# Two-layer hybrid trunk on one core: split weights get buffers 64 bytes longer, and start at the beginning or 64 bytes on, by stage

## The chip, the core and the metric

The kernel runs on one core of a Trainium2 chip, as one launch. The metric is the device time of one execution in microseconds (us). Before the change, three runs took 753.79, 753.91 and 755.08 us; the median is 753.91 us.

## What is computed

The input x is 256 tokens by 1024 features. Two layers follow each other, each of two sublayers. Cut to what matters:

```python
def hybrid_mixer(x, w_in, w_branch_sb, w_branch_moba, w_out):
    proj = x @ w_in                     # q,k,v of 8 + 8 heads, and two gates
    ...
    branch_sb = merge_heads(o_sb) @ w_branch_sb
    branch_mb = merge_heads(o_mb) @ w_branch_moba
    merged = jax.nn.sigmoid(g_sb) * branch_sb + jax.nn.sigmoid(g_mb) * branch_mb
    return merged @ w_out

for l in range(DEPTH):                  # 2
    mix = hybrid_mixer(x, ...)
    x = layer_norm(DEEPNORM_ALPHA * x + mix, ...)
    ffn = (silu(x @ w_gate) * (x @ w_up)) @ w_down      # 2816 wide
    x = layer_norm(DEEPNORM_ALPHA * x + ffn, ...)
```

Everything is float32. The matrix products work on pairs of float32r parts: a value is split into hi (rounded) and lo (the rest), and a product is hi·hi + hi·lo + lo·hi, three matmuls.

## The kernel before

**Weights.** All weights of a layer lie in HBM as 122 granules of 128 x 1024 float32, in the order of use (`_granules`). `WeightStream` brings them in one by one: a DMA from the SP queue into one of 4 raw buffers (`load`), a cast on ScalarE into `whi` (line 48), a subtraction on VectorE into `wlo` (line 53). There are 10 buffers for `whi` and 10 for `wlo` (`NSPLIT`); granule g takes the buffers that granule g - 10 has left. Every use of a granule is a set of `mm3` calls, three matmuls each, all recorded at line 275.

**Stages of a layer, by granule** (the names are those of the accumulators in PSUM, after l0 or l1):

- 0 to 7: `pv`, `pq` (in layer 1 both are called `pvq`), token-major. x is the stationary operand, 128 x 128, and a granule's 512 columns move through.
- 8, 9, 14, 15, 20, 21, 24, 25: `pqk`; 22, 23 and 26 to 39: `pg` (gates). Feature-major: the granule is stationary, 128 x 128, and x moves, 256 tokens wide (`feat_major`).
- 10 to 13 `pk` and 16 to 19 `pu`: token-major, 512 columns of weights move.
- 40 to 47: `pb`, the branch projections, feature-major: the granule is stationary, the attention output o moves, 256 wide.
- 48 to 55: `pw`, the output projection: m is stationary, 512 columns of weights move.
- 56 to 63: `pft`, the first chunks of SwiGLU, token-major, 512 columns move.
- 64 to 99: `pf`, the rest of SwiGLU, feature-major, x moves, 256 wide: 36 granules, 864 matmuls a layer.
- 100 to 121: the down projection, `pd` (and `pe` in layer 1): h is stationary, 512 columns of weights move, in two of `pe`'s banks 256.

The token-major stages on x (`pv`, `pq` or `pvq`, `pk`, `pu`, `pft`) have 288 matmuls a layer, `pb` has 192.

**Order.** Every engine takes its instructions in program order. `Weave` writes that order: the main line is the matmuls above, and side lines (attention heads, norms, rotary, the splits of the weights) are put between them by an estimate of when their operands are there. So matmuls of attention (`sb_s`, `mb_s`, `sb_o`, `mb_o`) and transposes (`pT`, `tp`, `sg..T`, line 288) interrupt the runs of projections at fixed places of the program.

**Where things lie.** A partition of SBUF is filled pool after pool, in the order in which the pools and their tiles are declared, each tile rounded up to 32 bytes. In the built program the constants begin at byte 16512 (129 x 128) with `ident` (512 bytes), `rope` (256), `x0` and `x1` (4096 each), `xT_hi` and `xT_lo` (8192 each) and `mask` (1024): all begin on a multiple of 128 bytes, x transposed (`xT_hi`, `xT_lo`) at 25472 and 33664. Then come `zero` and `mhalf`, 32 bytes each. So all that follows begins 64 bytes past a multiple of 128: the raw buffers from 42944, `whi` from 59328, `wlo` from 100288, and from 141248 the activations (o, m, h, q, k, v), 4096 bytes each. Slices inside a buffer are steps of 512 bytes and more. Call the first 64 bytes of each aligned 128 the lower half and the others the upper half: x transposed begins in the lower half, all weights and those activations begin in the upper half.

Of the kernel before, what the change touches and what calls it, by code (L numbers as in the profile page):

```python
# [8 lines left out]
F32R = mybir.dt.float32r  # L9
# [5 lines left out]
P = 128  # L15
# [14 lines left out]
GCOLS = 1024  # L30
NG_LAYER = 122
# [3 lines left out]
class Weave:  # L35
    """Program order: the main line of projections, with side lines (attention, norms,
    rotary, weight splits) woven in. Every engine takes its instructions in program order,
    so each is emitted about when its operands are there, by an estimate of the time at
    which each engine gets through what it has been given. A side line yields the time
    at which it goes on; on the tensor engine's clock."""  # L40

# [40 lines left out]
    def start(self, gen):  # L82
        """A side line whose first stage comes now."""
        side = self.add(gen)
        if not self.busy:
            self._step(side)
        return side
# [9 lines left out]
class WeightStream:  # L97
    """Weight granules [128, 1024]: loaded in float32, then split exactly into
    two float32r parts (hi = rounded, lo = the rest) for the tensor engine."""

# [13 lines left out]
    def load(self, upto):  # L114
        while self.loaded < min(upto, self.total):
# [7 lines left out]
            self.loaded += 1  # L123

    def line(self):
        """The side line: a granule at a time, as far as the buffers allow."""
        nc, weave = self.nc, self.weave
        while self.split < self.total:
            g = self.split
            ahead = g - self.current  # L130
            if g > self.limit:
                yield weave.t + 0.1
                continue
            if ahead >= LEAD and max(weave.dve_t, weave.act_t) > weave.t + BACKLOG:
                yield weave.t + 0.2
                continue
            self.load(g + NRAW)
            if ahead > 0:
                yield self.there[g]
            hi, lo = (self.pool.tile([P, GCOLS], F32R, tag=n, name=f"{n}{g}", bufs=NSPLIT)  # L140
                      for n in ("whi", "wlo"))
            t = self.raw.pop(g)
            n = GCOLS // len(self._pieces(g))
            for sl in self._pieces(g):
                e = weave.act(self.there[g], n, nc.scalar.copy, hi[:, sl], t[:, sl])
            if g - self.current > 0:
                yield e
            for sl in self._pieces(g):
                e = weave.dve(e, n, nc.vector.tensor_sub, lo[:, sl], t[:, sl], hi[:, sl].bitcast(F32))
            self.parts[g], self.ready[g] = (hi, lo), e  # L150
            self.split += 1
            self.load(g + 1 + NRAW)

    def allow(self, g):
        """Granule g's buffers are free from here on."""
        self.limit = max(self.limit, min(g, self.total - 1))
# [9 lines left out]
NRAW = 4  # L166
NSPLIT = 10
HOLD = 8
N_WARM = 7
# [10 lines left out]
def hybrid_trunk_kernel(ctx: ExitStack, tc: tile.TileContext, w, xT_in, x_in, ln_in,  # L180
# [6 lines left out]
    work = ctx.enter_context(tc.tile_pool(name="work", bufs=3))  # L187
# [24 lines left out]

# [1 line left out]
    xT_raw = [unit(f"xT_raw{t}", [P, KC, P]) for t in range(2)]  # L214
# [12 lines left out]
    nc.scalar.activation(warm, zero, AF.Sigmoid)  # L227
    # The tensor engine's clock rises after some microseconds of work: give it zeros meanwhile.
    idle = unit("idle", [P, 512], F32R)
# [42 lines left out]

# [1 line left out]
    def mm(o, a, b, start, stop):  # L274
# [30 lines left out]
    def tok_major(o, g, t, first, last, k0):  # L305
        """o[tokens of t, 512] += x @ granule g ([2 kc, 512])."""
        hi, lo = ws.take(g)
        hi = hi.rearrange("p (k c) -> p k c", k=2)
        lo = lo.rearrange("p (k c) -> p k c", k=2)
        for k in range(2):  # L310
            ts = slice(t * P, (t + 1) * P)
            mm3(o, xT_hi[:, k0 + k, ts], xT_lo[:, k0 + k, ts], hi[:, k, :], lo[:, k, :],
                first and k == 0, last and k == 1)

    def both_tokens(name, g0, put):
        """All tokens of x @ granules g0..g0+3; put(tokens, bank) takes each half."""
        acc = [bankM(f"{name}{t}", [P, WIDTH]) for t in range(2)]
        order = ((0, 0), (1, 0), (0, 1), (1, 1), (0, 2), (0, 3)) if g0 == 0 else \
            ((0, 0), (0, 1), (0, 2), (1, 0), (1, 1), (0, 3))
        for t, k in order + ((1, 2), (1, 3)):  # L320
            tok_major(acc[t], g0 + k, t, k == 0, k == 3, 2 * k)
            if t == 1:
                ws.allow(g0 + k + NSPLIT)
            if k == 3:
                put(t, acc[t])

    def feat_major(o, g):
        """o[128 columns, 256 tokens] = (x @ granule g)^T, g [8 kc, 128 columns]."""
        hi, lo = ws.take(g)
        hi = hi.rearrange("p (k c) -> p k c", k=KC)  # L330
        lo = lo.rearrange("p (k c) -> p k c", k=KC)
        for k in range(KC):
            mm3(o, hi[:, k, :], lo[:, k, :], xT_hi[:, k, :], xT_lo[:, k, :], k == 0, k == KC - 1)
        ws.allow(g + NSPLIT)

    def token_out(o, g, t, s_hi, s_lo, first, last):
        """o[tokens of t, 1024] += s^T @ granule g ([1 kc, 1024]); o: (first column, bank) ..."""
        hi, lo = ws.take(g)
        ts = slice(t * P, (t + 1) * P)
        for c0, ps in o:  # L340
            cs = slice(c0, c0 + ps.shape[-1])
            mm3(ps, s_hi[:, ts], s_lo[:, ts], hi[:, cs], lo[:, cs], first, last)

    ROWS = [(slice(h * DH, (h + 1) * DH), slice((1 - h) * DH, (2 - h) * DH)) for h in range(2)]

    # Per head, q is stacked as [hi; lo] over the 128 rows and each part of k is there twice,
    # so that q k^T = q_stack (k_hi twice) + q_stack (k_lo twice).
    def stack_q(qs, src, n, c, e):
        """qs[head] [128, ...] from src [2 heads x 64, ...]; the second head is [lo; hi]."""
        for h, (a, b) in enumerate(ROWS):  # L350
            e = act(e, n, nc.scalar.activation, qs[h][a], src[a], AF.Copy, scale=c)
        yield e
        for h, (a, b) in enumerate(ROWS):
            dve(e, n, nc.vector.scalar_tensor_tensor, qs[h][b], src[a], c, qs[h][a].bitcast(F32),
                op0=OP.mult, op1=OP.subtract)
# [15 lines left out]
    def rope_line(name, ps, t, put):  # L371
        """Token-major q or k (8 heads x 64) -> rotary -> transposed, handed to put."""
        tmp = work.tile([P, 8, DH], F32, tag="T", name=f"{name}_tok{t}")
# [22 lines left out]
    def scores(s, q, kh, kl, m):  # L396
        """Scores of both heads of a pair: columns 0:128 = (q0, k0), 128:384 = (q1, k0 k1),
        with the causal mask m added to the diagonal blocks."""
        for h in range(2):
# [12 lines left out]
    def weighted(name, p, wt, v, oT, e):  # L412
        """oT[:, p] = (wt @ v)^T for both heads of pair p."""
        yield e + MARGIN
# [93 lines left out]
    def scale_shift(e, x, cols, sub, op, scale, g, b, e_scale):  # L508
        """x <- ((x op sub) g) scale + b; yields each piece of columns as it is done."""
        for c in cols:  # L510
# [7 lines left out]
    def norm_line(name, t, junk, gb):  # L518
        """x_t <- LN(alpha x_t + ps) g + b, and its transpose into xT (split)."""
        x = xs[t]  # L520
# [26 lines left out]
    def last_norm(name, t, banks, gb, down):  # L547
        """The output's tokens: LN(alpha x_t + sum) g + b, blocks of columns in turn."""
        x = xs[t]
# [24 lines left out]

# [1 line left out]
    norms = []  # L576
    for l in range(DEPTH):
        G = l * NG_LAYER
        L = f"l{l}"

        # v of stick-breaking and q of MoBA: tokens 0..127 first
        v_sb = pair_tiles(L + "vsb", [P, 2, WIDTH])
# [28 lines left out]

        # Each pair of stick-breaking heads starts with its q and k; k and v of MoBA and the
        # first gates come between, MoBA's heads after the last sigmoid of stick-breaking, and
        # the gates' sigmoids after the last exponential of MoBA.
        o_sb = pair_tiles(L + "osb", [P, NPAIR, S])
# [47 lines left out]

        # branch projections and the gated merge, feature-major
        gb = load_gb(l, 0)
# [20 lines left out]

        # output projection: tokens 0..127 first
        norms = []
# [7 lines left out]

        # SwiGLU, first chunks token-major (tokens 0..127 first)
        h_t = [pair_tiles(f"{L}h{i}", [P, 4, S]) for i in range((NFC + 3) // 4)]
# [47 lines left out]

        # down projection: the last granules' tokens 0..127 first
        gb = load_gb(l, 1)
# [108 lines left out]
```

## Time and profile before

| | |
|---|---|
| runs | 753.79, 753.91, 755.08 us; median 753.91 |
| profiled execution, span from first to last instruction | 747.6 us |
| median of the runs less that span | 6.3 us |
| instructions | 12689, of these 5049 matmuls |
| matmul time that the page shows as busy | 735.1 us, 98% of the span |
| VectorE, ScalarE busy | 71%, 56% |
| share of the chain of waits that is matmul | 84% |

The profile gives the span, and no separate time of the execution around it. A matmul's own duration in it holds its way through the array (276 to 283 ns for 256 columns); as matmuls follow each other in a pipeline, the pace is read from the distance of their starts. In the chain of waits a piece such as "143.10 23.02 PE l0pb L275 x192" gives the start, the duration and the number of the matmuls in it, and duration by number is the pace.

### The profile page before, as it was taken

The page shows a single profiled execution, that of the slowest core. Times are in us where ns is not written, and L with a number is a line of the kernel's source. Part 1 is how long each engine was busy: PE and PEld are TensorE (multiplying, and loading weights), DVE is VectorE, ACT ScalarE, POOL GpSimd, SP SyncE. Part 2 cuts the span into 40 slices and gives each one's busy share as a digit, 9 for nine tenths or more (in the row PEclk, how much of TensorE's full clock was granted, in tenths as well). Part 3 has the DMA queues.
Part 4 walks back from the last instruction along what each step waited for, and adds up shares of the span by engine and source line. Part 5 has one row for each costly group of instructions (what it writes and reads, how often), then busy time and mean ns, then how long its engine had stood idle before and what let it go on. Part 6 is the DMA issues. An engine that isn't in the chain of part 4 may idle for free.

```text
span 747.6 us, 12689 instructions
## 1 busy us (share of the span) xinstructions
PE 735.1 (98%) x5049; PEld 675.5 (90%) x5049; DVE 529.9 (71%) x772; ACT 421.8 (56%) x655; POOL 13.4 (2%) x20
## 2 busy tenths in 40 slices
PE   8999999999999999999999999999999999999996
PEld 5888999998799999988888889999987999999885
DVE  6897878696886666644488878886768866665416
ACT  6788867744565445433267877777435654554300
POOL 0000000000000000000000000000010000000001
PEclk9999999999999999999999999999999999999999
DMA  8864724554586565676168445345635865657501
GB/s 292 284 217 151 221 93 153 176 199 167 178 265 227 181 194 182 198 241 194 60 196 258 146 162 177 108 145 198 210 113 183 277 201 194 196 185 246 166 1 56
DMA packets 39082, 136.31 MB, mean 182 GB/s; under 512 B 4464, under 2 KB 6000, under 8 KB 39024
## 3 DMA queue, kind: packets, MB, share of 16 engines
q1 hardware_dynamic: 39024, 135.51, 55.6%
q8 instruction: 39, 0.64, 0.3%
q14 instruction: 19, 0.16, 0.1%
HBM read 134.45 MB, written 1.05 MB: 181 GB/s over the span
## 4 chain that ended last, share of the span: by engine, by line
PE 84%; DVE 6%; ACT 3%; DMA 3%; issue 2%; POOL 1%; SPq 0%; POOLq 0%; DVEq 0%; ACTq 0%
PE l0pf L275 14%; PE l1pf L275 13%; PE l0pd L275 8%; PE l1pg L275 6%; PE l0pg L275 6%; PE l1pe L275 4%; PE l1pd L275 4%; PE l1pb L275 3%; PE l0pb L275 3%; PE l1pvq L275 3%; DMA raw<-in_w_dram 3%; PE l1pw L275 2%; PE l0pw L275 2%; PE l1pqk L275 2%; DVE wlo L53 2%
## 5 line engine op out<-in xcount | busy, mean ns | idle before, releaser
L53 DVE TENSOR_TENSOR wlo<-raw,whi 128x1024 fp32r<-128x1024 f32 (+1 forms) x245 | 296.8, 1219 | 93.0 <-ACT whi L48 89.5
L48 ACT CAST whi<-raw 128x1024 fp32r<-128x1024 f32 (+1 forms) x245 | 254.1, 1046 | 86.7 <-PE l0pd L275 22.6
L275 PE MATMUL l0pf<-xT_hi,whi 128*128 128x256 f32 x288 | 81.0, 281 | 0.0
L275 PE MATMUL l0pf<-xT_lo,whi 128*128 128x256 f32 x288 | 80.9, 281 | 0.0
L275 PE MATMUL l0pf<-xT_hi,wlo 128*128 128x256 f32 x288 | 80.9, 281 | 0.0
L275 PE MATMUL l1pf<-xT_hi,whi 128*128 128x256 f32 x288 | 79.6, 276 | 0.0
L275 PE MATMUL l1pf<-xT_lo,whi 128*128 128x256 f32 x288 | 79.5, 276 | 0.0
L275 PE MATMUL l1pf<-xT_hi,wlo 128*128 128x256 f32 x288 | 79.5, 276 | 0.0
L275 PEld LDWEIGHTS l0pf<-xT_hi,wlo 128*128 128x128 f32 x288 | 55.3, 192 | 0.0
L275 PEld LDWEIGHTS l0pf<-xT_lo,whi 128*128 128x128 f32 x288 | 54.1, 188 | 0.0
L275 PEld LDWEIGHTS l1pf<-xT_lo,whi 128*128 128x128 f32 x288 | 54.1, 188 | 0.0
L275 PEld LDWEIGHTS l0pf<-xT_hi,whi 128*128 128x128 f32 x288 | 54.1, 188 | 0.0
L275 PEld LDWEIGHTS l1pf<-xT_hi,whi 128*128 128x128 f32 x288 | 54.1, 188 | 0.0
L275 PEld LDWEIGHTS l1pf<-xT_hi,wlo 128*128 128x128 f32 x288 | 54.1, 188 | 0.0
L275 PE MATMUL l0pg<-xT_hi,whi 128*128 128x256 f32 x128 | 35.9, 281 | 0.0
L275 PE MATMUL l1pg<-xT_hi,whi 128*128 128x256 f32 x128 | 35.9, 281 | 0.0
L275 PE MATMUL l0pg<-xT_lo,whi 128*128 128x256 f32 x128 | 35.5, 277 | 0.0
L275 PE MATMUL l1pg<-xT_lo,whi 128*128 128x256 f32 x128 | 35.5, 277 | 0.0
L275 PE MATMUL l1pg<-xT_hi,wlo 128*128 128x256 f32 x128 | 35.4, 277 | 0.0
L275 PE MATMUL l0pg<-xT_hi,wlo 128*128 128x256 f32 x128 | 35.4, 277 | 0.0
L275 PE MATMUL l0pd<-whi,l0h_hi 128*128 128x512 f32 x88 | 34.4, 391 | 0.0
L275 PE MATMUL l0pd<-whi,l0h_lo 128*128 128x512 f32 x88 | 34.3, 389 | 0.0
(379 smaller groups left out, 1821.1 us busy)
## 6 DMA issues: line engine op xcount, KB each, us to landing
raw<-in_w_dram SPq DMA_DIRECT2D x243, 512.0 KB, 4.1
ln<-in_ln_dram SPq DMA_DIRECT2D x8, 512.0 KB, 7.3
xT_raw<-in_xT_dram SPq DMA_DIRECT2D x8, 128.0 KB, 5.0
x<-in_x_dram SPq DMA_DIRECT2D x2, 512.0 KB, 6.4
out_dram<-x SPq DMA_DIRECT2D x3, 256.0 KB, 2.1
raw<-in_w_dram SPq DMA_DIRECT2D x2, 256.0 KB, 3.7
out_dram<-x SPq DMA_DIRECT2D x2, 128.0 KB, 2.0
mask<-in_mask_dram SPq DMA_DIRECT2D x1, 128.0 KB, 3.2
```

What stands on the lines that cost most here:

```text
L48: f(*args, **kw)
L53: f(*args, **kw)
L275: nc.tensor.matmul(o, a, b, start=start, stop=stop)
```

## The change

Each of the 20 split buffers becomes a tile of its own (a tag for each, one buffer to a tag), of 1040 instead of 1024 columns, 4160 bytes. The granule's 1024 columns are a slice of it, from column 0 or from column 16 (64 bytes on). `EVEN` lists the granules of a layer of which `whi` begins at 16 and `wlo` at 0; for the others it is the other way round. No instruction is added or removed; the buffer of granule g is still that of g modulo 10.

```diff
+    def _part(self, n, g):
+        t = self.pool.tile([P, GCOLS + LINE], F32R, tag=f"{n}{g % NSPLIT}", name=f"{n}{g}", bufs=1)
+        k = g % NG_LAYER
+        even = any(a <= k < b for a, b in EVEN)
+        at = LINE if even == (n == "whi") else 0
+        return t[:, at:at + GCOLS]
...
-            hi, lo = (self.pool.tile([P, GCOLS], F32R, tag=n, name=f"{n}{g}", bufs=NSPLIT)
-                      for n in ("whi", "wlo"))
+            hi, lo = (self._part(n, g) for n in ("whi", "wlo"))
...
 NSPLIT = 10
+LINE = 16
+EVEN = ((0, 8), (10, 14), (16, 20), (40, 48), (56, 64))
```

The rest of the diff blanks comments and docstrings and leaves the line numbers as they were.

The tags are met in the order whi0, wlo0, whi1, wlo1 and so on. With 4160 bytes each (65 x 64), `whi` of buffer i begins at 59328 + 8320 i, in the upper half, and `wlo` at 4160 more, in the lower half. So for a granule in `EVEN` both parts begin in the lower half, where x lies, and for all others both begin in the upper half, as all do before. Twenty buffers are 20 x 64 = 1280 bytes (10 x 128) longer together, so the halves of everything behind them stay as they were.

| stage | columns that move | other operand | weights before | weights after |
|---|---|---|---|---|
| pv, pq, pvq, pk, pu, pft | 512, of weights | x, lower | upper | lower |
| pqk, pg, pf | 256, of x | x, lower | upper | upper |
| pb | 256, of o | o, upper | upper | lower |
| pw, pd, pe | 512 and 256, of weights | m or h, upper | upper | upper |

## The prediction

> **What bounds the kernel now.** First the page: span, engines, clock and the shares of the chain of waits.
>
> ```profile
> span 747.6 us, 12689 instructions
> ...
> PE 735.1 (98%) x5049; PEld 675.5 (90%) x5049; DVE 529.9 (71%) x772; ACT 421.8 (56%) x655; POOL 13.4 (2%) x20
> ...
> PEclk9999999999999999999999999999999999999999
> ...
> PE 84%; DVE 6%; ACT 3%; DMA 3%; issue 2%; POOL 1%; SPq 0%; POOLq 0%; DVEq 0%; ACTq 0%
> ```
>
> TensorE never lacks work for long, at full clock. So the time is the number of matmuls by their pace, and the change can act only through the pace. I took it from the chain in order of time, in which an unbroken run of matmuls is one piece (start, duration, what, number):
>
> ```profile
> 77.56 5.44 PE l0pg L275 x48
> ...
> 83.92 5.65 PE l0pqk L275 x48
> ...
> 143.10 23.02 PE l0pb L275 x192
> 166.12 17.04 PE l0pw L275 x75
> ...
> 198.69 4.82 PE l0pft L275 x21
> ...
> 215.20 99.64 PE l0pf L275 x846
> 314.84 55.08 PE l0pd L275 x243
> ...
> 391.39 7.57 PE l1pvq L275 x33
> ...
> 511.20 23.02 PE l1pb L275 x192
> ...
> 583.38 95.90 PE l1pf L275 x846
> ```
>
> Duration by number, for 256 moving columns: `pg` 113.3 ns, `pqk` 117.7, `l0pf` 117.8, `l1pf` 113.4, `pb` 119.9 in both layers. For 512: `pft` 229.5, `pvq` 229.4, `pw` 227.2, `pd` 226.7. The shapes are equal, the paces are not. Set beside where the operands begin, they fall into groups. With 256 columns, `pb` has weights and activations in the same half and is slowest; `pg`, `pqk`, `pf` have them in opposite halves and go at one of two paces, 113.4 or 117.8. With 512 columns it is turned round: `pw` and `pd`, same half, are faster than `pft` and `pvq`, opposite halves. The weight loads, which run beside the stream of the matmul before, show the meeting (shortest, median, longest duration):
>
> ```profile
> L275 PEld LDWEIGHTS l0pb<-l0osb_hi,whi x32: 188/192/192, 142.8 to 164.0; 128*128 128x128 f32 x32
> ...
> L275 PEld LDWEIGHTS l0pg<-xT_hi,whi x128: 187/188/192, 77.3 to 142.5; 128*128 128x128 f32 x128
> ```
>
> In `pb` nearly every load takes 192 ns, in `pg` 188: load and stream delay each other there. I therefore read the pace as set by where stream and load stand against each other within 128 bytes, with a rhythm that, once found, is kept until something interrupts.
>
> **What the change moves.** No instruction, DMA or wait is added or removed; the buffers turn over as before, so the queues carry the same order. Two groups of stages change their relation, the others keep it.
>
> **pb** (384 matmuls): from the same half to opposite halves. Its pace becomes that of the opposite-half rows: 113.3 (`pg`) or 117.8 (`l0pf`). Per layer 23.02 us becomes 192 x 113.3 = 21.75 or 192 x 117.8 = 22.62; the gain for both layers is 2.5 us or 0.8 us. I take 2.5: `pb` follows `pg` with no break between them, and `pg` is in the fast rhythm then, as both streams change halves together.
>
> **Token-major stages on x** (576 matmuls): from opposite halves to the same. Ceiling: 229.4 - 226.7 = 2.7 ns x 576 = 1.6 us. But the fast pace is not there at once. After transposes, same half (`pw`, first fence) and opposite (`pft`, second), start of each matmul in the timeline:
>
> ```profile
> 185.19 0.48 PE L275 MATMUL l0pw<-whi,l0m_hi 128*128 128x512 f32 x1
> 185.50 0.40 PE L275 MATMUL l0pw<-wlo,l0m_hi 128*128 128x512 f32 x1
> ...
> 187.59 0.39 PE L275 MATMUL l0pw<-wlo,l0m_hi 128*128 128x512 f32 x1
> ```
>
> ```profile
> 203.49 0.48 PE L275 MATMUL l0pft<-whi,xT_hi 128*128 128x512 f32 x1
> 203.81 0.40 PE L275 MATMUL l0pft<-wlo,xT_hi 128*128 128x512 f32 x1
> ...
> 205.88 0.39 PE L275 MATMUL l0pft<-wlo,xT_hi 128*128 128x512 f32 x1
> ```
>
> From the first to the eleventh start it is 2.40 us in the one and 2.39 in the other: ten matmuls after an interruption nothing is gained. The timeline cuts these stages into runs between interruptions, such as these two:
>
> ```profile
> 62.17 3.00 PE l0pu L275 x12
> ...
> 66.08 4.13 PE l0pu L275 x18
> ```
>
> Counting in each run what lies past the tenth: layer 0 about 50 in `pv` and `pq`, 16 in `pk`, 23 in `pu`, 60 in `pft`; layer 1 about 60 in `pvq` and the same in the others; together some 310 of 576. I leave out the 50 in `l0pv` and `l0pq`, where the chain goes through arriving weights, the last of them this piece:
>
> ```profile
> 25.24 5.17 DMA raw<-in_w_dram
> ```
>
> 260 x 2.7 = 0.7 us; the ends are 0, if the rhythm is never found, and 1.6.
>
> **The splits** write and read the moved slices. The nearest rows: a VectorE subtraction of 256 columns from an upper-half source into the lower half (`xT_lo`), and one all in the upper half (`l0m_lo`); the casts likewise.
>
> ```profile
> L53 DVE TENSOR_TENSOR l0m_lo<-l0mt,l0m_hi 128x256 fp32r<-128x256 f32 x8 | 3.4, 420 | 0.8 <-ACT l0m_hi L48 0.8
> ...
> L53 DVE TENSOR_TENSOR xT_lo<-xT_raw,xT_hi 128x256 fp32r<-128x256 f32 x8 | 3.0, 419 | 2.3 <-ACT xT_hi L48 2.3
> ```
>
> ```profile
> L48 ACT CAST l0m_hi<-l0mt 128x256 fp32r<-128x256 f32 x8 | 3.2, 406 | 10.3 <-DVE l0mt L53 10.3
> ...
> L48 ACT CAST xT_hi<-xT_raw 128x256 fp32r<-128x256 f32 x8 | 2.9, 404 | 1.8 <-DMA xT_raw<-in_xT_dram 1.8
> ```
>
> 419 against 420 ns and 404 against 406: nothing, and both engines have a quarter or more of the span free to cover a nanosecond.
>
> **pf, which is not moved, can still change.** Two transposes (`sg11T`) interrupt it after 18 matmuls; then 846 follow unbroken. In layer 0 that run fell into the slow rhythm, in layer 1 into the fast one, with the same halves: 99.64 - 95.90 = 3.74 us between them. The starts show how near the choice is, layer 0 first:
>
> ```profile
> 214.95 0.36 PE L275 MATMUL l0pf<-xT_hi,whi 128*128 128x256 f32 x1
> 215.15 0.28 PE L275 MATMUL l0pf<-xT_lo,whi 128*128 128x256 f32 x1
> 215.27 0.28 PE L275 MATMUL l0pf<-xT_hi,wlo 128*128 128x256 f32 x1
> ```
>
> ```profile
> 583.14 0.37 PE L275 MATMUL l1pf<-xT_hi,whi 128*128 128x256 f32 x1
> 583.34 0.28 PE L275 MATMUL l1pf<-xT_lo,whi 128*128 128x256 f32 x1
> 583.46 0.28 PE L275 MATMUL l1pf<-xT_hi,wlo 128*128 128x256 f32 x1
> ```
>
> Both begin 0.20 and then 0.12 us apart. `pft`, just before, now arrives in another rhythm, so both layers draw anew. Runs behind four or six transposes in other 256-column stages were fast (114.2, 114.0 and 113.6 ns):
>
> ```profile
> 72.74 2.74 PE l0pqk L275 x24
> ...
> 103.03 3.42 PE l0pg L275 x30
> ...
> 458.69 3.75 PE l1pg L275 x33
> ```
>
> Of the two behind a pair of transposes one was slow. I take one slow and one fast again, 0; the ends are -3.7 us (both fast) and +3.7 (both slow).
>
> **Sum.** On the span: 747.6 - 2.5 - 0.7 = 744.4 us. The 6.3 us between the span and the median of the runs I carry over: 753.9 - 3.2 = **750.7 us**.
>
> **A rule against it.** The Trainium skill (SBUF — State Buffer, Who interferes with whom) gives TensorE two independent read ports, one for the stream and one for weight loads, and says that "PE and ACT never wait on anyone". By it a load cannot slow a stream wherever both lie, and the change is worth 0. The loads of 192 against 188 ns speak against it; no run here has yet moved an operand alone.
>
> **The rivals.**
>
> 1. *Placement is not the cause.* `pb` may be slow because its moving operand changes tile every 12 matmuls, and `pft` because of its neighbours; `l0pf` and `l1pf` differ by 4.4 ns at the same placement, so something else does set paces. Against: the two groups are turned round between 256 and 512 columns without one exception. Time 753.9, within 1 us. The rule of the two ports in the Trainium skill, above, would give the same.
> 2. *The rhythm depends on more than 128 bytes.* Before, all same-half operands are a multiple of 512 bytes apart, so the trace cannot tell; buffers of 4160 bytes leave multiples of 128. If 256 counts, half of the token-major gain fails, and half of the 512-column matmuls of `pw`, `pd` and `pe` (some 650 by the code) lose 2.7 ns: 753.9 - 2.5 - 0.35 + 0.9 = 751.9.
> 3. *Both pf fast*: 750.7 - 3.7 = 747.0. For it: transposes usually lead to the fast rhythm. Against: a pair did so once in two.
> 4. *pb finds the slow rhythm*, pf as before: 753.9 - 0.8 - 0.7 = 752.4. For it: score matmuls in front of `l0pqk` left 48 at 117.7.
> 5. *The other side: both pf slow.* The place is the pair of transposes in `l1pf`; if the third matmul behind it starts like that of layer 0, 846 matmuls take 3.74 us more: 750.7 + 3.7 = 754.4, and with the slow rhythm in `pb` 756.1. It decides as soon as `l1pf` alone turns, since 3.7 is more than the 3.2 gained. For it: the very same code did it in layer 0.
>
> **How the numbers follow.** Forecast 0.34; placement no cause 0.12; longer period 0.06; both pf fast 0.27; `pb` slow 0.08; both pf slow 0.13. A measurement of this kernel tells about 0.2% (1.5 us) from no change, so faster means under 752.4 and slower over 755.4. Faster: 0.34 + 0.27, half of rivals 2 and 4 (0.07) and nothing else = 0.68. Slower: the worse half of rival 5, 0.06, and 0.01 of rival 1 = 0.07. Same: the rest, 0.25. The range reaches down to both pf fast and up to one step over no change, 746.8 to 754.4; the forecast's own is 749.8 to 751.4, from the ends of the token-major term.
>
> **What would show it.** In the chain of the changed kernel, `l0pb` and `l1pb` should be about 21.8 us for 192 matmuls, and their loads 188 ns; 23.0 refutes the step, 22.6 is rival 4. Unbroken stretches of `pft` and `pvq` should come to 226.7 ns after some ten matmuls; 229 refutes it. `pd`, `pw` should stay at 226.7, else rival 2 holds. `l0pf` and `l1pf` should be 99.6 or 95.9 for 846, in either order; a third value, or `whi` casts and `wlo` subtractions longer than now, would make the prediction wrong in a way that I did not see.

## The result, and the profile after

The changed kernel takes 747.57 us (median of four runs, 747.13 to 749.20), the kernel before 753.88 us beside it (753.79 to 755.08). The ratio is 0.9915, with a 95% interval of 0.990 to 0.993: 0.85% or 6.3 us faster, twice the 3.2 us that were forecast.

Executions of the kernel before are of two kinds, some near 750 us and most near 754, and all four beside the changed kernel were of the longer kind; the changed kernel has one kind.

The page of the changed kernel first: span, engines and clock (what line 275 is in the kernel before is line 286 here).

```profile
span 745.4 us, 12689 instructions
...
PE 732.9 (98%) x5049; PEld 670.4 (90%) x5049; DVE 530.3 (71%) x772; ACT 421.8 (57%) x655; POOL 13.4 (2%) x20
...
PEclk9999999999999999999999999999999999999999
```

The same instructions, the same clock, TensorE busy for the same share. The span is only 2.2 us shorter than that of the profile before (747.6), while the runs are 6.3 us shorter: the first thing to clear up. This execution took 747.87 us, so 2.5 us lie outside its span, not 6.3.

Next the chain of waits of the changed kernel, in order of time (start, duration, what, number):

```profile
144.39 21.98 PE l0pb L286 x192
166.37 17.31 PE l0pw L286 x75
...
199.18 4.86 PE l0pft L286 x21
...
215.82 95.92 PE l0pf L286 x846
311.74 56.09 PE l0pd L286 x243
...
389.38 7.64 PE l1pvq L286 x33
...
509.32 21.97 PE l1pb L286 x192
531.29 17.31 PE l1pw L286 x75
...
580.80 95.92 PE l1pf L286 x846
```

Four things stand here beside the rows of before. `pb` is 21.98 instead of 23.02 us, within a quarter of a microsecond of the forecast's 21.75. Both `pf` are 95.92. `pw` and `pd`, which were to keep their pace, are slower: 17.31 for 17.04 and 56.09 for 55.08. And the token-major stages on x, which were to gain, lost a little: `pft` 4.86 / 21 = 231.4 ns (229.5 before), `pvq` 7.64 / 33 = 231.5 (229.4 before).

The weight loads by group (busy us, mean ns of one), again of the changed kernel:

```profile
L286 PEld LDWEIGHTS l0pf<-xT_hi,wlo 128*128 128x128 f32 x288 | 54.1, 188 | 0.0
...
L286 PEld LDWEIGHTS l0pb<-l0osb_hi,whi 128*128 128x128 f32 x32 | 6.0, 188 | 0.0
```

`pb`'s loads went from 192 to 188 ns as its matmuls came closer together. The fast rhythm is not there at once: by the starts in the timeline, the first 48 matmuls of `l0pb` come 117.7 ns apart and all that follow 113.3. The rule of the Trainium skill (SBUF — State Buffer, Who interferes with whom) that stream and loads have ports of their own and TensorE waits for nobody does not agree with that: nothing but addresses differs between the two kernels.

### The profile page after: what moved, and what is told of

It is laid out like the page before. It is cut to its first block, busy times and chain, and to the rows that moved or that the text cites. A ratio compares the mean times of both kernels' runs of the same rounds, so it can differ in the third digit from the quotient of the medians.

```text
span 745.4 us, 12689 instructions
## 1 busy us (share of the span) xinstructions
PE 732.9 (98%) x5049; PEld 670.4 (90%) x5049; DVE 530.3 (71%) x772; ACT 421.8 (57%) x655; POOL 13.4 (2%) x20
## 4 chain that ended last, share of the span: by engine, by line
PE 85%; DVE 5%; ACT 4%; DMA 3%; issue 2%; POOL 1%; SPq 0%; POOLq 0%; DVEq 0%; ACTq 0%
PE l1pf L286 13%; PE l0pf L286 13%; PE l0pd L286 8%; PE l0pg L286 6%; PE l1pg L286 6%; PE l1pe L286 4%; PE l1pd L286 4%; PE l1pvq L286 3%; PE l0pb L286 3%; PE l1pb L286 3%; DMA raw<-in_w_dram 3%; PE l1pw L286 2%; PE l0pw L286 2%; PE l1pqk L286 2%; PE l0pft L286 2%; PE l1pft L286 2%
## 5 line engine op out<-in xcount | busy, mean ns | idle before, releaser
L53 DVE TENSOR_TENSOR wlo<-raw,whi 128x1024 fp32r<-128x1024 f32 (+1 forms) x245 | 296.7, 1219 | 92.5 <-ACT whi L48 89.2
L286 PE MATMUL l0pd<-wlo,l0h_hi 128*128 128x512 f32 x88 | 34.5, 393 | 0.0
```

Of the source, the lines that this page charges most:

```text
L53: f(*args, **kw)
L286: nc.tensor.matmul(o, a, b, start=start, stop=stop)
```

## Where 6.3 us outside the span came from: more profiles of before

Nothing is edited in these runs; they are the kernel before, in five more runs (the first with ten executions, the others with one each).

> The kernel before, unchanged, run again, for its span beside its time. The change moved the profiled span by 2.2 us and the time by 6.3. Theory A (rhythm of pf): the profiled execution of before was an unusual one, whose l1pf had the fast rhythm; the timed executions of before have both pf in the slow one. Then the spans of the timed executions here are about 751.3 us, some 2.5 less than their times, and l0pf and l1pf each take 99.6 us for 846 matmuls. Theory B (something outside the span): the spans are 747.6 and the times 753.9, 6.3 apart, as the first profile said.

> The kernel before, unchanged, for one more profile. If the longer executions are those with both pf stages slow: an execution of 753.4 to 755.3 us has a span of 751 to 753 and l0pf and l1pf 99.6 us each; one of 749.5 to 751.5 has l0pf 99.6 and l1pf 95.9. If the 3.7 us lie outside the span or in the beginning, l1pf is 95.9 in both kinds.

> A further profile of the kernel before, with the same two expectations: l1pf 99.6 us where the execution takes over 753 us, or 95.9 in both kinds.

> A further profile of the kernel before, with the same two expectations: l1pf 99.6 us where the execution takes over 753 us, or 95.9 in both kinds.

> A further profile of the kernel before, with the same two expectations: l1pf 99.6 us where the execution takes over 753 us, or 95.9 in both kinds.

Measured: the first has a median of 753.52 us and a ratio of 0.9988 (0.9966 to 1.001); its ten executions are 749.81, 749.95, 750.37, 751.35 and six from 753.43 to 755.27. The four single executions are 753.63, 750.67, 749.74 and 750.61 us, with spans of 751.2, 748.2, 747.6 and 748.5. The first of these four fell on the longer kind. Its chain:

```profile
143.38 23.02 PE l0pb L275 x192
...
215.48 99.64 PE l0pf L275 x846
315.12 55.08 PE l0pd L275 x243
...
511.15 23.02 PE l1pb L275 x192
534.17 17.04 PE l1pw L275 x75
...
583.28 99.64 PE l1pf L275 x846
```

And the chain of the second, which is of the shorter kind:

```profile
215.90 99.64 PE l0pf L275 x846
...
584.05 95.90 PE l1pf L275 x846
```

So the two kinds differ in `l1pf`, by 3.74 us; `l0pf` was slow in all six profiles. Outside the span lie 2.1 to 2.5 us in these four, whatever the kind. Of the 77 timed executions of the kernel before on record, 30 were of the shorter kind (749.51 to 752.25 us, spans of 747.3 to 749.4) and 47 of the longer (753.36 to 756.15 us, spans of 751.0 to 754.0). The profile that the prediction was made from was of the shorter kind, the three times beside it were of the longer. Against the shorter kind, whose median is 750.4 us, the changed kernel gains 2.8 us and not 6.3.

What is slow in a slow `pf` shows in its loads, by group, in the longer execution:

```profile
L275 PEld LDWEIGHTS l1pf<-xT_hi,wlo 128*128 128x128 f32 x288 | 55.3, 192 | 0.0
...
L275 PEld LDWEIGHTS l1pf<-xT_lo,whi 128*128 128x128 f32 x288 | 54.1, 188 | 0.0
...
L275 PEld LDWEIGHTS l1pf<-xT_hi,whi 128*128 128x128 f32 x288 | 54.1, 188 | 0.0
```

One load in three takes 192 ns, the other two 188; in `pb` of before all three take 192, in the fast `pf` of the changed kernel none does. The three matmuls of a product repeat, and in this slow rhythm it is the same one of the three whose load is long each time.

Against that longer execution the changed kernel's span can be added up, stage by stage, from the chains above (span 751.2 to 745.4):

| stretch | longer execution of before | changed | difference |
|---|---|---|---|
| start to `l0pb` | 143.38 | 144.39 | +1.01 |
| `pb`, both layers | 46.04 | 43.95 | -2.09 |
| `pw`, both layers | 34.08 | 34.62 | +0.54 |
| between `pw` and `pf`, with `pft`, both | 64.10 | 64.34 | +0.24 |
| `pf`, both layers | 199.28 | 191.84 | -7.44 |
| `l0pd` | 55.08 | 56.09 | +1.01 |
| `l0pd` to `l1pb`, with `pvq` | 140.95 | 141.49 | +0.54 |
| end of `l1pf` to the end, with `pd`, `pe` | 68.28 | 68.68 | +0.40 |

Together -5.8. The first stretch, in which arriving weights set the pace, ended at 143.10 to 144.12 us in the six profiles of before, so most of its +1.01 need not be the change.

## The experiments

**The changed kernel again**, to see whether it too has two kinds.

> The changed kernel once more, beside the run before this, on the same chip. Theory (the long buffers free pf for good): pf 95.9 in both layers, times within 747 to 749.5 with no jump of 3.7, median about 747.6. Rival (pf was fast by chance in the first executions): some executions at 751 or above.

Measured: 747.14 us, 747.04 to 747.88 in six executions, ratio 0.9922 (0.9898 to 0.9946). Its profile has `l0pf` at 95.92 and `l1pf` at 95.90. One kind, both `pf` fast.

**Longer buffers, nothing moved by stage.** The list of granules is empty, so `wlo` always begins 64 bytes on and `whi` never does; the 4160-byte buffers stay.

```diff
-EVEN = ((0, 8), (10, 14), (16, 20), (40, 48), (56, 64))
+EVEN = ()
```

> The changed kernel with an empty EVEN: buffers of 4160 bytes, all weights in the upper half, none moved to the other half. It isolates what the longer buffers alone do. Theory A (pf freed by the longer buffers): both pf are fast (95.9 us), pd slow (56.1 for 243), pb about 120 ns (22 to 23.0 us), token-major near 230 ns; time about 748 to 750, most of the gain without any placement. Theory C (the halves are what counts): pf as before, time near 753.9.

Measured: 748.93 us, ratio 0.9935 (0.992 to 0.995), no executions of a second kind. Its chain:

```profile
143.37 22.77 PE l0pb L286 x192
166.15 17.31 PE l0pw L286 x75
...
215.61 95.89 PE l0pf L286 x846
311.50 56.09 PE l0pd L286 x243
```

Most of the gain, 4.9 us of the 6.3, comes without any placement by stage. The longer buffers, with `wlo` 64 bytes on, free `pf` and slow `pw` and `pd` by themselves. The placement adds most of `pb`'s gain: 22.77 to 21.98, 1.6 us for both layers.

**Placement by stage, without the scatter.** Nine buffers of 4608 bytes, so that every buffer begins at the same place modulo 512; once with nothing moved, once with the granules in `EVEN` moved by 448 bytes (64 back, modulo 512). In the first `EVEN` is empty as well.

```diff
-NSPLIT = 10
+NSPLIT = 9
+PAD = 128
+SHIFT = 112     # 0 in the first of the two
...
+        t = self.pool.tile([P, GCOLS + PAD], F32R, tag=f"{n}{g % NSPLIT}", name=f"{n}{g}", bufs=1)
...
-        at = LINE if even == (n == "whi") else 0
+        at = SHIFT if even else 0
```

> Nine instead of ten pairs of split buffers, each of 4608 bytes (9 x 512), nothing moved: every weight begins in the upper half and all stand a multiple of 512 bytes from each other and from the activations, as before the change. It is the control for the next run. If nine buffers do as well as ten: paces of before (pb 119.9, pd 226.7, token-major 229, pf 113.3 or 117.8 by chance) and a time within 1 us of before. If ten are needed, waits of TensorE for wlo appear and the time rises.

> As the run with nine buffers, but the granules of EVEN begin 448 bytes on in both parts, so that in token-major stages weights and x stand a multiple of 512 bytes apart, and in pb 64 less. This is the placement that the prediction had in mind, without the scatter over 128 bytes that buffers of 4160 bytes bring. If the pace follows from the distance alone: pb 113.3 ns (21.8 us), long token-major runs 226.7 ns, pd stays at 226.7; 3.2 us better than the control by the prediction's own sum, apart from pf, which can go either way by 3.7 us a layer. If it does not: token-major stays at 229 to 231.

Measured: 760.48 us with nothing moved (759.68 to 761.18, ratio 1.009, 1.0074 to 1.0107; one buffer fewer, nothing else moved), 753.65 us with the granules moved (ratio 1.0001, 0.9971 to 1.0032). But the latter's executions lie in three steps, 749.4, 752.8 to 753.8 and 756.4 to 759.3: by the size of the steps none, one or both `pf` slow. Compared where both `pf` are slow, as in both profiles, it is 760.08 to 756.66 us, a gain of 3.4. From the chain with nothing moved:

```profile
143.76 23.02 PE l0pb L288 x192
...
395.23 8.26 PE l1pvq L288 x36
```

From the chain of the moved one:

```profile
143.02 21.76 PE l0pb L288 x192
164.78 17.04 PE l0pw L288 x75
...
204.09 5.49 PE l0pft L288 x24
...
215.61 99.64 PE l0pf L288 x846
315.25 55.11 PE l0pd L288 x243
...
393.14 8.19 PE l1pvq L288 x36
```

This is the change as the prediction understood it. `pb` is 21.76 (forecast 21.75), `pw` and `pd` are unmoved. The token-major step is there as it was described: by the starts in the timeline, from the tenth matmul after an interruption on, `pft` and `pvq` go at 226.8 to 226.9 ns in the pieces of 24 and 36 matmuls above, where the control has 228.8 to 229.2. But it is small: 8.19 for 8.26 us, 5.49 for 5.52, about 0.2 us over all unbroken pieces of `pft` and `pvq`, of a forecast 0.7 that counts `pk` and `pu` too. That the whole comes to 3.4 us for 3.2 is in part luck: of the 3.3 us between the spans (757.8 and 754.5), 2.5 are `pb` and 0.74 lie ahead of `l0pb` (143.76 to 143.02), where profiles of one and the same kernel differ by up to 1.02. What the real change does beyond that is the work of the 4160 bytes. And `pf` still draws its rhythm here.

**The same, moved by 64 bytes forward**, so that weights and x are 128 apart instead of at the same place, and o is 64 from the weights on the other side.

```diff
-SHIFT = 112
+SHIFT = 16
```

> As the run with nine buffers and 448 bytes, but the granules of EVEN begin 64 bytes on in both parts: in token-major stages weights and x are then 128 bytes apart within 512 instead of 0. If the period is 128 bytes: token-major 226.7 ns in long runs, as at 448. If it is 256 or more: another pace, about 229 to 233. pb at 113.3 either way (64 on one side or the other).

Measured: one execution, 752.59 us. Its chain:

```profile
143.84 22.61 PE l0pb L288 x192
...
205.82 5.58 PE l0pft L288 x24
```

`pft` at 5.58 / 24 = 232.5 ns is slower than at 64 apart (5.52, 230.0) and slower still than at the same place (5.49, 228.8). If places counted within 128 bytes, 128 apart would be the same place. The period is longer than 128 bytes: that was rival 2. `pb` went to 22.61 / 192 = 117.8 ns, the slow rhythm, so 64 bytes on is not the same as 64 bytes back, which had been expected to be equal.

**Which part frees pf: x or the weights?** In the changed kernel the `whi` and `wlo` of a granule in `pf` begin 128 bytes apart, modulo 256. Three edits of the kernel before, each with pads only, shown together with notes (the third has a second pad behind the `wlo` buffers, as behind x): the lo part of x 128 bytes on, both parts of x 128 bytes on, and all `wlo` buffers 128 bytes on.

```diff
+    const.tile([P, 32], F32, name="pad0")        # ahead of xT_lo; in the second ahead of xT_hi
     xT_lo = const.tile([P, KC, S], F32R, name="xT_lo")
+    const.tile([P, 96], F32, name="pad1")        # what follows keeps its place
...
+            if g == 0:                           # the third: between the whi and the wlo buffers
+                self.pool.tile([P, 32], F32, tag="pad0", name="pad0", bufs=1)
```

> The kernel before with 128 unused bytes between xT_hi and xT_lo and 384 behind xT_lo (so that all else keeps its place within 512 bytes). Weights are not touched. Theory (scatter frees pf): the slow rhythm of pf needs all three matmuls of a group at one distance within 256 bytes; if x's lo part stands 128 bytes aside, it cannot hold. Then l0pf and l1pf take 95.9 us for 846 in every execution, pb stays at 23.0 and pd at 55.1, the times no longer jump, and the median is 753.8 - 2 x 3.74 = 746.3 us, less or more by up to 1.3 for the token-major stages, which read x too. Rival (pf is freed by something else in the changed kernel, such as the order of buffers): pf as before, 99.6 in most executions, time near 753.8.

> The kernel before with 128 unused bytes ahead of xT_hi and 384 behind xT_lo: both parts of x move 128 bytes on, weights and activations keep their places within 512 bytes. Let d be where the stationary operand begins less where the moving one does, within 512. Then in pqk, pg and pf d goes from +64 to -64, in the token-major stages from -64 to +64. Theory (the sign of d decides: with 256 columns -64 is fast for good, as in pb of the run at 448 bytes with 113.3 ns, and +64 has two rhythms, as in pf and in pb of the run at 64 bytes with 117.8): pf takes 95.9 us in both layers and in every execution, pb 23.0, pd 55.1; the times no longer jump, and the median is 753.8 - 2 x 3.74 = 746.3 us, by up to 1.5 more if +64 is worse than -64 for 512 columns. Rival (a distance of 64 either way has two rhythms, and chance decides): pf at 95.9 or 99.6 by execution, times that jump by 3.7 between 746 and 754.

> The kernel before with 128 unused bytes between the buffers of whi and those of wlo (and 384 behind): 10 buffers of 4096 bytes each, all whi at one place within 512 bytes, all wlo 128 further. It takes one part of the scatter of the 4160-byte buffers alone. Theory (the distance of 128 between the parts does both): pf free (95.9), pd slowed to about 230 ns (56 us for 243), pb between 22.0 and 23.0; time about 748 to 749, like the longer buffers without placement (748.9). Rival (what counts is the step from granule to granule): pd stays at 55.1 and pf at 99.6 or by chance.

Measured: lo part of x, 757.84 us (757.46 to 759.23; ratio 1.008, 1.0053 to 1.0107). Both parts of x, 758.10 us (ratio 1.0066, 1.0044 to 1.0089). All `wlo`, 750.52 us (749.32 to 752.26; ratio 0.998, 0.9957 to 1.0003, on a chip where the kernel before was of the shorter kind half of the time). None of the three shows a second kind; the last is 1.5 us over the upper end of its expectation. From the chain with the lo part of x moved:

```profile
78.20 5.66 PE l0pg L277 x48
...
217.35 99.64 PE l0pf L277 x846
...
587.47 99.64 PE l1pf L277 x846
```

From the chain with all `wlo` moved:

```profile
143.79 22.87 PE l0pb L279 x192
166.66 17.50 PE l0pw L279 x75
...
216.21 95.92 PE l0pf L279 x846
312.13 56.69 PE l0pd L279 x243
...
582.71 95.89 PE l1pf L279 x846
```

I had expected that setting either lo part aside would break the rhythm. Setting x aside does the contrary: both `pf` are at 99.64 in either profile, no execution of the two runs is a step of 3.7 us lower, and `pg` joins them (5.66 for 5.44). With both parts of x aside the loads of the slow `pf` are not the long ones (shortest, median and longest in ns):

```profile
L277 PEld LDWEIGHTS l1pf<-xT_hi,wlo x288: 187/188/188, 585.0 to 686.6; 128*128 128x128 f32 x144
```

The other two of the three matmuls have medians of 187 and 188. So loads of 192 ns go with the slow pace in the kernel before, and the same pace comes without them here. That a load and a stream delay each other is therefore one reading of the kernel before and not a shown cause; what is shown is that addresses set the pace. Two theories fell here, that only the distance of hi and lo counts, and that the sign of the step between stationary and moving operand does. Setting the stationary lo aside frees `pf` in every execution, as far as the times show it, and costs in `pw` and `pd` (17.50 and 56.69) what the scatter of the changed kernel costs, and more.

**Only where it helps.** The kernel before, with `wlo` buffers 128 bytes longer, whose tile begins 128 bytes aside (modulo 256) for listed granules alone; in one run for the feature-major granules, in the other for `pf`'s only.

```diff
+            lo = self.pool.tile([P, GCOLS + LINE], F32R, tag=f"wlo{i}", name=f"wlo{g}", bufs=1)
...
+            aside = any(a <= k < b for a, b in ASIDE)
+            at = LINE if aside != (i % 2 == 1) else 0
+            lo = lo[:, at:at + GCOLS]
...
+LINE = 32
+ASIDE = ((8, 10), (14, 16), (20, 48), (64, 100))      # the other run: ((64, 100),)
```

> The kernel before, with hi buffers as they are and each lo buffer 4224 bytes long, its tile set so that it begins 128 bytes on (counted in 256) in the feature-major stages qk3, pg's branch projections, pb and pf, and 0 bytes on in the token-major ones (pvq, pw, pft, pd). If a stage's pace hangs on where operands begin within 256 bytes: l0pf and l1pf 95.9 us both, in every execution; pb 22.87 (as the run with all lo parts 128 bytes on had it); pd 55.1 and pw 17.04, as before; the median 753.8 - 7.5 (pf) - 0.3 (pb) - 0.2 (pqk3) = about 745.8 us, under the changed kernel's 747.1 to 747.6. If it hangs on where they begin within 512 bytes, or on the step from one buffer to the next: pd and pw do not come back to 55.1 and 17.04 but stay near 56.5 and 17.4, and the median is 747.5 to 749. If what freed pf was only the scatter of hi too: pf 99.6, and about 753.

> The same, with the lo tiles 128 bytes on for pf's 36 granules of a layer alone. If the other stages' rhythm before pf decides what pf does: pf in one of two paces, the median anywhere from 746 to 754. If pf's own operands decide: l0pf and l1pf 95.9 us both in every execution, pb 23.02 as before, and the median about 753.8 - 7.5 = 746.3 us.

Measured: 747.12 us (746.77 to 747.25; ratio 0.9933, 0.9908 to 0.9959) and 747.05 us (745.67 to 748.78; ratio 0.994, 0.9917 to 0.9964), beside a kernel before that was mostly of its shorter kind there, at a median of 750.66. The chain of the first:

```profile
144.44 22.87 PE l0pb L284 x192
167.31 17.05 PE l0pw L284 x75
...
216.42 95.89 PE l0pf L284 x846
312.31 55.10 PE l0pd L284 x243
...
580.53 95.90 PE l1pf L284 x846
```

And of the second, where `pb` is left alone:

```profile
143.12 23.02 PE l0pb L284 x192
...
215.23 95.89 PE l0pf L284 x846
...
579.31 95.90 PE l1pf L284 x846
```

Both `pf` are fast, with `pw` and `pd` back at the pace of before, although successive `wlo` buffers now lie 4224 bytes apart: the place within 256 bytes decides, not the step between buffers. Moving `pf`'s own weights is enough to set its rhythm, with all that runs ahead of it left as it was. The first run came out 1.3 us over its expectation; its rows put 1.1 us of that ahead of `l0pb` (144.44 against 143.38 in the longer execution of before), in the stretch of arriving weights; the cause of that is open. Neither run is told from the changed kernel (747.1 to 747.6): `pb` is slower than there, `pd` and `pw` are faster, and by the rows the two about cancel.

**All at once, at the price of a raw buffer.** Ten pairs of 8704 bytes, clean modulo 512 and moved as in the run with nine, need room: three raw buffers instead of four.

```diff
-NRAW = 4
+NRAW = 3
...
+PAD = 128
+SHIFT = 112
...
+        t = self.pool.tile([P, 2 * GCOLS + PAD], F32R, tag=f"w{g % NSPLIT}", name=f"w{g}", bufs=1)
...
+        at = SHIFT if any(a <= k < b for a, b in EVEN) else 0
+        return t[:, at:at + GCOLS], t[:, at + GCOLS:at + 2 * GCOLS]
```

> Ten split buffers again, in clean steps: whi and wlo of a granule in one tile of 8704 bytes (17 x 512), both 448 bytes on for the granules of EVEN; the room comes from 3 instead of 4 raw buffers. The placement that was predicted, without nine buffers' waits. If three raw buffers are enough: pb 21.8, pd 55.1, token-major 226.7, and the time is 753.8 - 3.2 = 750.6 with both pf slow, 3.7 less for each that is fast. If not: TensorE waits for whi and wlo, and the time is above 753.8.

Measured: 759.78 us (757.74 to 762.62; ratio 1.0103, 1.0061 to 1.0145). The chain of it, from `l0pb` on:

```profile
146.57 21.78 PE l0pb L283 x192
...
172.20 4.64 DMA raw<-in_w_dram
...
178.03 1.24 DVE w L53
```

`l0pb` is 21.78, as fast as without the scatter, but behind it the chain leaves TensorE and goes through an arriving granule and its split; matmuls are 74% of this chain, where they were 84 to 89% in the six profiles of before. The clean placement is not worth a raw buffer.

## Why the prediction was right and wrong

- **pb: right.** Forecast 21.75 us a layer with loads at 188 ns, measured 21.98 and 188; without the scatter 21.76. The 0.2 between them is the first 48 matmuls, which go at 117.7 ns before the fast rhythm is found.
- **The carry-over: wrong, and the main error.** "The 6.3 us between the span and the median of the runs I carry over" took a difference between two kinds of execution for a fixed cost. Of the 6.3 us, 3.74 were `l1pf` in its slow rhythm and some 2.2 to 2.5 lay outside the span. The profile and the times shown were not of the same kind, and the profile had both paces of `pf` in it, 99.64 and 95.90, exactly 3.74 us apart: the prediction quoted that number and did not hold it against the 6.3. In the sum, 744.4 + 6.3 was forecast and the profiled execution is 745.4 + 2.5. That the span came within 1 us is itself partly luck: `pf` gave 3.7 us that the sum did not have, and 3.6 us lost elsewhere, 1.3 of them ahead of `l0pb`, took them back.
- **pf, "draws anew", taken at 0: wrong.** In the changed kernel no draw is seen. The placement that the change gives it without meaning to, `whi` and `wlo` 128 bytes apart modulo 256, goes with the fast pace in both layers in both profiles, and no time of the ten executions is a step higher: -7.44 us against the longer kind, -3.7 against the shorter. The step looked at which half of 128 bytes the operands lie in, found it unmoved and stopped.
- **Rival 3 (both `pf` fast, 747.0)** gave nearly the time, 747.57, partly by luck: it counted one `pf` instead of two (3.7 us too little), and the losses elsewhere, which it did not have, made up for most of that.
- **Token-major on x, -0.7: wrong for this change.** They were to come to 226.7 ns and are at 231 and more in the chain. With x and weights at the same place modulo 512 the pace of 226.8 does come after ten matmuls, but the gain that the chain shows is about 0.2 us for `pft` and `pvq`. In the changed kernel the 4160-byte buffers put half the granules at the same place as x modulo 256 and half 128 bytes away, where the pace is 232.5.
- **"The others keep it": wrong for `pw`, `pd`, `pe`.** Rival 2 named the mechanism (a period over 128 bytes, buffers a multiple of 128 apart) and priced it at 0.9 us; the stretches of `pw`, `l0pd` and the end lost 0.54 + 1.01 + 0.40 = 1.95.
- **The reading behind the steps, that load and stream meet within 128 bytes: not borne out.** The period is longer than 128 bytes, and with both parts of x 128 bytes aside `pf` is slow though the median of its loads is 187 to 188 ns.
- **The splits, 0: right.** The subtraction into `wlo` takes 1219 ns on the page before and after, the cast 1046.

Rival 1, that placement is not the cause, is out: kernels with the same instructions in the same order, differing in pads alone, run from 750.5 to 758.1 us, and moving the `wlo` of `pf` alone frees both `pf`.

**What stays open** is a rule for the rhythm. In steps of 64 bytes modulo 256, with the stationary operand first: 256 columns take 113.4 or 117.8 ns at (3, 2); 117.8 at (3, 0) and (0, 3); 113.3 at (2, 3); 119.9 at (3, 3); and 113.4 with hi at (3, 2) and lo at (1, 2). The entries (0, 3) and (2, 3) rest on one profile each. No function of the distance modulo 256 alone gives that table. The place is not all either: in the changed kernel `pb`'s granules alternate between (0, 3) and (2, 3), and after the first two both go at 113.3. And what settles the draw at (3, 2), which in the kernel before fell slow in `l0pf` six times in six and both ways in `l1pf`, was not found.

## What to carry to other kernels

Before a time is predicted from a profile, hold the profiled execution's span against the times of the runs: here 2.1 to 3.2 us lay outside the span, and a gap of 6.3 was the hint that the two were of different kinds, while a stage that appears twice at two paces said where to look. When a kernel is bound by the pace of back-to-back matmuls, the pace of each shape (duration by number in the chain) is worth a table: the spread between equal shapes, here up to 6%, is there to be won by placement in SBUF, without an instruction changed. And a pad put in to move one thing moves the buffers behind it as well: work out where every operand begins, modulo 256 and not only modulo 128, before a stage is called unmoved.

## What was not expected of the hardware

- A stage of 846 matmuls keeps one of two paces, 113.4 or 117.8 ns, from its beginning to its end. In the slow one of the kernel before every third weight load takes 192 instead of 188 ns, but with both parts of x 128 bytes aside the pace is as slow and the median of the loads is 187 to 188. The same code falls into either from one execution to the next, and a kernel's time so has steps of 3.7 us.
- With the weights' lo part 128 bytes on, both `pf` were fast in every profile, and with x's lo part 128 bytes on both were slow (95.9 against 99.64 us); no execution of either has a time of the other kind.
- With 512 moving columns the order is another: 226.7 ns at the same place modulo 256 (`pd`), 229 to 230 at 64 bytes, 232.5 at 128 bytes (`pft`).
